# A Mamba-2 layer of a hybrid encoder: the splits of weight blocks are scheduled 140 instructions ahead instead of 60

## The chip, the cores and the metric

The kernel runs on one core of a Trainium2 chip, in one launch. The metric is the device time of one execution in microseconds (us). The engines are named as in the profile: PE (TensorE, with PEld for its weight loads), DVE (VectorE), ACT (ScalarE), POOL (GpSimd) and SP (SyncE, which here only issues transfers).

## The reference

The reference is an encoder trunk of two layers for one sequence of 512 tokens, 1024 wide, in float32. Layer 0 runs a bidirectional retention and a 2-D neighbourhood attention side by side, layer 1 a bidirectional Mamba-2 mixer; each layer ends with a GeGLU block. The mixer of layer 1, where the change is, computes per direction a chunked scan (chunks of 128 tokens, 4 groups of 8 heads, state 128):

```python
def step(h, inp):
    qq, kk, vv, aa = inp
    cs = jnp.cumsum(aa, axis=1)
    seg = cs[:, :, None] - cs[:, None, :]
    decay = jnp.exp(jnp.where(mask[None, :, :, None, None], seg, -jnp.inf))
    qk = jnp.einsum('bjgn,blgn->bjlg', qq, kk)
    y_intra = jnp.einsum('bjlgh,blghp->bjghp', qk[..., None] * decay, vv)
    y_inter = jnp.einsum('bjgn,bghnp->bjghp', qq, h) * jnp.exp(cs)[..., None]
    tail = jnp.exp(cs[:, -1:] - cs)
    h_new = h * jnp.exp(cs[:, -1])[..., None, None] + jnp.einsum('blgn,blghp->bghnp', kk, vv * tail[..., None])
    return h_new, y_intra + y_inter
```

Ahead of it stand a projection to z, x, B, C and the step sizes, a centred convolution of width 5 over x, B and C with a SiLU, and a softplus of the step sizes; behind it a gate with silu(z), a grouped RMSNorm and the output projection.

## The kernel before

Activations and weights are kept in two halves for PE's products in the type fp32r: `hi` is the cast of a float32 block, `lo` what the cast left over. A product of two blocks is three matmuls (`mm3`, L104 to L106): hi x hi, lo x hi, hi x lo. One of 512 columns starts every 0.22 us or so, and 24 of them (8 blocks of the 1024 rows, three each) make one tile of a projection.

A weight block comes in three steps. `wload` (L64) has SP load 128 x 1024 floats into a staging tile `wst`; `split` has ACT cast it to `whi` (L95) and VectorE subtract to `wlo` (L96). `wunit` does all three and puts the split into `tc.high_priority(60)`: the scheduler, which builds every engine's list of instructions at compile time, takes the two instructions as if they stood 60 instructions of the program earlier than where the kernel writes them. The load is not moved by that, it goes as early as its buffer allows. There are 3 staging buffers, 4 for high halves and 4 for low halves, and 4 accumulators `mm` and 4 small ones `px` in PSUM. An engine works through its list in order, so an instruction that waits holds up all that stand behind it.

`mixer1` is the Mamba-2 mixer. It works through four groups of 8 heads. The projection of a group has ten units: unit 0 is B, unit 1 is C, 2 to 5 are x, 6 to 9 are z. `project` makes a unit's weights, its 24 products, and for units under 6 the convolution: one ACT instruction (L754) and four of VectorE (L757). `silus` applies the SiLU to all tiles that are pending, the first as L763 (with a load of ACT's table if another function was in use), the rest as L766, and has B and x transposed by PE (L737, copied out by ACT at L738). For one group, `state` makes the state of one chunk and direction (VectorE L791, PE L793, ACT copies the first state of a direction at L796, VectorE L799 and L801 do the later ones); `head` turns one head's decays into a mask: ACT adds per-chunk offsets to a row of decays that a transfer has spread over the partitions (`pb`, L823, eight instructions), VectorE puts the other direction in by a copy under a mask (L825), ACT takes the exponential (L827) and issues the next load of `pb` (L812), and VectorE multiplies by the products of B and C (L829); `inter` and `pair` make the outputs (PE L844 and L864). The order of these pieces is written out by hand, one string per group (`SLOTS`): t is a unit of the own group, n one of the next, S and N their silus, s a state, h a head, i and p the outputs, o the output projection of the group before. Group 0 begins with

```python
"G s0 s1 t6 t7 s2 i0 h0 t8 t9 S h1 p0 i1 n0 h2 h4 h3 p1 i2 n6 n1 h5 n7 i3 n9 p2 N n3 n4 n2 n5 h6 h7 p3 n8 N",
```

Ahead of the groups, `mixer1` projects units 0 to 2 of group 0, calls `steps()`, and projects units 3, 4 and 5. `steps()` makes from the step sizes all that the scans need: a softplus as a polynomial on VectorE (L302 to L307), the running sum of the log decays (`pf`, a scan at L689), its exponentials on ACT (`ysc` and `sw`, L712 to L715), the table `tok` by PE transposes (L725) of two tiles, one with a logarithm (Ln, L720) and one the product `sw` (L717). It writes the running sums and `ysc` to DRAM (`pd`, L710, and `yd`, L716), and the loads of `pb` (the first three on SP, L812) and of `gain` (L836) read them back spread over the partitions. The numbers behind the names in the rows further down are the program's buffer numbers: whi_5978 holds the weights of n0 (unit 0 of group 1, projected in group 0's row of `SLOTS`), whi_6126 those of n1, whi_5860 and whi_5892 those of t8 and t9; mm_5982 is n0's accumulator and z_5921, z_5778, z_5810, z_5889 are the z tiles of group 0.

Of the kernel before, what the change touches and what calls it, by code (L numbers as in the profile page):

```python
# [26 lines left out]
class Env:  # L27


    def __init__(self, ctx, tc):  # L30
# [27 lines left out]
        self.xl = self.res.tile([P, KD, S], R32, name="xl")  # L58
        self.late, self.xs, self.turned = [], {}, {}

    def wload(self, src, behind=None):

        st = self.wst.tile([P, 1024], F32, name="wst")
        m = self.nc.sync.dma_start(st, src)  # L64
        if behind:
            self.together([m], [behind])
        return st

    def wunit(self, src, parts=None, st=None, behind=None, low_behind=None):

        if st is None:
            st = self.wload(src)
        halves = slice(0, 512), slice(512, 1024)
        if parts is None:
            hi, lo = self.whi.tile([P, 1024], R32, name="whi"), self.wlo.tile([P, 1024], R32, name="wlo")
            with self.tc.high_priority(60):
                self.split(hi, lo, st, behind, low_behind)
            return [(hi[:, c], lo[:, c]) for c in halves]  # L80
        with nullcontext() if behind else self.tc.high_priority(60):
            for j, c in enumerate(halves):
                self.split(parts[j], parts[j + 2], st[:, c], behind)
        return [(parts[j], parts[j + 2]) for j in range(2)]
# [537 lines left out]
def mixer1(E, w_dt, w_fm, cw, dtc, cols, mask, w_out, g_post_row, done, ahead):  # L622
# [8 lines left out]
    with ExitStack() as ctx:  # L631
# [102 lines left out]
        def to_tok(src, dst):  # L734
            pt = E.px.tile([P, NT, P], F32, name="pt", tag="px")
            for c in range(NT):
                nc.tensor.transpose(pt[:, c], src[:, c * C:(c + 1) * C], E.ident)  # L737
            nc.scalar.copy(dst, pt)  # L738
# [21 lines left out]
        def silus(o):  # L760

            r, src, i = o["silu"][-1]
            lead = nc.scalar.activation(r, src, AF.Silu)  # L763
            with tc.issue_after(lead.ins):
                for r, src, _ in o["silu"][:-1]:
                    nc.scalar.activation(r, src, AF.Silu)  # L766
            for r, _, i in o["silu"]:
                o["t"][i] = r
                if i == 0:
                    o["bt"] = one.tile([P, NT, P], F32, name="bt")  # L770
                    to_tok(r, o["bt"])
                elif 2 <= i < 6:
                    if "x" not in o:
                        o["x"] = two.tile([P, NT, 512], F32, name="xt")
                    to_tok(r, o["x"][:, :, (i - 2) * P:(i - 1) * P])
            o["silu"] = []

        def products(o):
            pg = E.px.tile([P, NT, P], F32, name="pg", tag="px")
            for c in range(NT):  # L780
                cc = slice(c * C, (c + 1) * C)
                nc.tensor.matmul(pg[:, c], o["t"][0][:, cc], o["t"][1][:, cc], start=True, stop=True)
            o["gt"] = one.tile([P, NT, P], F32, name="gt")
            nc.scalar.copy(o["gt"], pg)

        def state(o, dr, i):

            g = o["g"]
            c = i if dr == 0 else NT - 1 - i
            xs = E.tmp.tile([P, 512], F32, name="xs", tag="tmp")  # L790
            nc.vector.tensor_tensor(hv(xs), hv(o["x"][:, c]), rows(1, dr, g, c), op=ALU.mult)  # L791
            ps = E.px.tile([P, 512], F32, name="st", tag="px")
            nc.tensor.matmul(ps, o["bt"][:, c], xs, start=True, stop=True)  # L793
            ns = one.tile([P, 512], F32, name=f"state{dr}{i}")
            if i == 0:
                nc.scalar.copy(ns, ps)  # L796
            else:
                h = dr * H + g * HPG
                nc.vector.tensor_tensor(hv(ns), hv(o["st"][dr, i - 1]), etot[:, h:h + HPG, c:c + 1].broadcast_to([P, HPG, 64]),  # L799
                                        op=ALU.mult)  # L800
                nc.vector.tensor_tensor(ns, ps, ns, op=ALU.add)  # L801
            o["st"][dr, i] = ns
# [12 lines left out]
        def head(o, j):  # L815

            g = o["g"]
            h = g * HPG + j
            pb = pbs.pop(0)

            for dr in range(2):
                for c in range(NT):
                    nc.scalar.activation(pb[:, dr, c], pb[:, dr, c], AF.Identity, scale=1.0 - 2 * dr,  # L823
                                         bias=tok[:, 0, c, dr * H + h:dr * H + h + 1])
            nc.vector.copy_predicated(pb[:, 1], um.bitcast(U32).rearrange("p (o l) -> p o l", o=1).broadcast_to([P, NT, C]), pb[:, 0])  # L825
            e = three.tile([P, NT, C], F32, name="e")
            nc.scalar.activation(e, pb[:, 1], AF.Exp)  # L827
            load(nc.scalar)
            o["m"][j] = e, nc.vector.tensor_tensor(e, e, o["gt"], op=ALU.mult)  # L829

        def inter(o, q):

            g = o["g"]
            ysc = E.gain.tile([P, 2, S], F32, name="gain")
            for j in range(2):
                nc.sync.dma_start(ysc[j * 64:j * 64 + 64],  # L836
                                  yd.rearrange("(r h) s -> h r s", r=2)[g * HPG + 2 * q + j].partition_broadcast(64))
            y = ys.tile([P, S], F32, name="y")
            d, x = col[:, 0, g * 4 + q:g * 4 + q + 1], o["t"][2 + q]
            for dr in range(2):  # L840
                pi = E.px.tile([P, 3, C], F32, name="pi", tag="px")
                for i in range(NT - 1):
                    c = i + 1 if dr == 0 else NT - 2 - i
                    nc.tensor.matmul(pi[:, c - 1 + dr], o["st"][dr, i][:, q * P:(q + 1) * P],  # L844
                                     o["t"][1][:, c * C:(c + 1) * C], start=True, stop=True)
                cc = slice(C, S) if dr == 0 else slice(0, S - C)
                ti = E.tmp.tile([P, 384], F32, name="ti", tag="tmp")
                nc.vector.tensor_tensor(ti, pi.rearrange("p c l -> p (c l)"), ysc[:, dr, cc], op=ALU.mult)
                if dr == 0:
                    nc.vector.tensor_scalar(y[:, :C], x[:, :C], d, None, op0=ALU.mult)  # L850
                    nc.vector.scalar_tensor_tensor(y[:, cc], x[:, cc], d, ti, op0=ALU.mult, op1=ALU.add)
                else:
                    nc.vector.tensor_tensor(y[:, cc], y[:, cc], ti, op=ALU.add)
            o["yi"][q] = y
# [45 lines left out]
        def rms(o):  # L900

            if "ss" in o:
                E.together([nc.vector.tensor_tensor(o["ss"], squares(o, o["sq"][1], o["sqw"][3:]), o["ss"], op=ALU.add)], [o["yl"]])
            else:
                part(o)
            o["r"] = E.small.tile([P, NT], F32, name="rg", bufs=2)
            nc.gpsimd.tensor_tensor(o["r"], o["ss"], E.mhalf.broadcast_to([P, NT]), op=ALU.pow)
# [27 lines left out]
        def out(o, n):  # L935
            ws = E.wunit(w_out[o["g"], n, 0]) + E.wunit(w_out[o["g"], n, 1])
            for t in range(NT):
                out_tile(o, n, t, ws)
# [5 lines left out]
            silus(o)  # L944

        w0 = [E.wunit(w_fm[0, i]) for i in range(3)]
        p0 = [E.mm.tile([P, S], F32, name="mm") for _ in range(3)]
        for c in range(2):
            for i, (w, ps) in enumerate(zip(w0, p0)):
# [11 lines left out]
        for g, o in enumerate(gs):  # L961
            nx = gs[g + 1] if g + 1 < NG else None
            for step in SLOTS[g].split():
                a, i = step[0], int(step[1:] or 0)
                if a == "G":
                    products(o)
                elif a == "o":
                    out(gs[g - 1], i)
                elif a == "s":
                    state(o, 0, i)  # L970
                    state(o, 1, i)
                elif a == "h":
                    head(o, i)
                elif a == "i":
                    inter(o, i)
                elif a == "p":
                    pair(o, i)
                elif a == "R":
                    rms(gs[g - 1])
                elif a == "t":  # L980
                    project(o, i)
                elif a == "n":
                    project(nx, i)
                else:
                    silus(o if a == "S" else nx)
        g_post = E.bcast(g_post_row)
        st = {}

# [179 lines left out]
```

## Time and profile before

| | us |
|---|---|
| three timed runs | 1412.8, 1414.03, 1415.81 |
| median of them | 1414.03 |
| the profiled execution's own time | 1413.29 |
| its span in the trace | 1411.5 |
| PE busy in the span | 1386.6 |
| DVE, ACT, POOL busy | 905.2, 710.1, 61.3 |
| mixer1, from the trace | about 600 to 1020 |

The span is what the trace covers; the execution's own time is 1.8 us more. Rows of the timeline read: start, duration, engine, line, operation, what it writes and reads, count, and in brackets how long the engine sat idle before it and what ended that. PE's matmuls are pipelined, so their durations overlap and the distance of two starts tells how fast they go. SPq and ACTq are transfers issued by these engines, with the time that the issuing took.

### The profile page before, as it was taken

How to read it: one execution, taken by the hardware profiler on the slowest of the kernel's cores; microseconds unless marked ns; L12 is line 12 of the kernel's file. 1: busy time of each engine (PE TensorE's matmuls, PEld its weight loads, DVE VectorE, ACT ScalarE, POOL GpSimd, SP SyncE). 2: the span in 40 equal slices, each digit the busy share in tenths (PEclk: the TensorE clock that was granted, in tenths of full speed). 3: DMA queues.
4: the chain of work that ended last, by engine and by line, in shares of the span. 5: the costliest groups of instructions: out<-in, count | busy, mean ns of one | idle time of the engine just before them, and what ended most of it. 6: DMA issues, size and time to landing. Idle time of an engine off the chain costs nothing.

```text
span 1411.5 us, 18022 instructions
## 1 busy us (share of the span) xinstructions
PE 1386.6 (98%) x6908; PEld 1145.5 (81%) x6908; DVE 905.2 (64%) x1364; ACT 710.1 (50%) x1203; POOL 61.3 (4%) x66
## 2 busy tenths in 40 slices
PE   7999999999999999999999999999999999999998
PEld 6878787898888888888778787887888888888886
DVE  7378787755666552447878686897786565654232
ACT  5356665444444431334878787487354444442230
POOL 0010110100000000000000010000110000000000
PEclk9999999999999999999999999999999999999999
DMA  8442233223233333323566454273433323232231
GB/s 291 149 144 91 87 98 106 89 77 96 99 96 99 95 89 114 109 109 110 138 186 191 135 183 145 78 207 110 132 120 104 104 90 105 90 104 91 90 105 60
DMA packets 56439, 166.36 MB, mean 118 GB/s; under 512 B 6688, under 2 KB 7456, under 8 KB 56352
## 3 DMA queue, kind: packets, MB, share of 16 engines
q1 hardware_dynamic: 48464, 150.00, 33.3%
q10 hardware_dynamic: 7888, 15.21, 3.9%
q8 instruction: 55, 0.90, 0.3%
q14 instruction: 32, 0.26, 0.1%
HBM read 157.57 MB, written 5.51 MB: 116 GB/s over the span
## 4 chain that ended last, share of the span: by engine, by line
PE 90%; DVE 4%; ACT 3%; issue 1%; DMA 1%; POOL 0%; DVEq 0%; SPq 0%; POOLq 0%; ACTq 0%
PE mm L104 27%; PE mm L106 27%; PE mm L105 27%; PE pi L844 1%; PE st L793 1%; PE py L864 1%; PE pt L161 1%; PE pt L737 1%; PE y L519 1%; ACT pb L823 1%; DMA pb<-pd 0%; DMA x<-in_x 0%; DVE wlo L96 0%; ACT whi L95 0%; PE y L580 0%
## 5 line engine op out<-in xcount | busy, mean ns | idle before, releaser
L106 PE MATMUL mm<-xl,whi 128*128 128x512 f32 (+2 forms) x1216 | 463.9, 382 | 2.8 <-DVE xl L96 2.8
L104 PE MATMUL mm<-xh,whi 128*128 128x512 f32 (+1 forms) x1216 | 464.7, 382 | 0.7 <-ACT xh L95 0.2
L105 PE MATMUL mm<-xh,wlo 128*128 128x512 f32 (+2 forms) x1216 | 463.5, 381 | 1.2 <-DVE wlo L96 1.2
L96 DVE TENSOR_TENSOR wlo<-wst,whi 128x1024 fp32r<-128x1024 f32 (+1 forms) x208 | 255.2, 1228 | 136.7 <-ACT whi L95 134.8
L95 ACT CAST whi<-wst 128x1024 fp32r<-128x1024 f32 (+1 forms) x208 | 216.6, 1042 | 146.1 <-PE mm L105 117.7
L106 PEld LDWEIGHTS mm<-xl,whi 128*128 128x128 f32 (+1 forms) x1216 | 228.8, 188 | 47.3 <-DVE xl L96 3.0
L104 PEld LDWEIGHTS mm<-xh,whi 128*128 128x128 f32 x1216 | 229.1, 188 | 45.6 <-issue 2.5
L105 PEld LDWEIGHTS mm<-xh,wlo 128*128 128x128 f32 (+1 forms) x1216 | 229.1, 188 | 44.4 <-DVE wlo L96 1.6
L251 DVE SCALAR_TENSOR_TENSOR cv<-mm,cwt,cv 128x511 f32<-128x511 f32 x88 | 65.9, 749 | 147.1 <-ACT cv L250 147.1
L250 ACT ACTIVATE cv<-mm,cwt 128x512 f32<-128x512 f32 x88 | 68.6, 780 | 125.5 <-PE mm L106 125.5
L104 PE MATMUL mm<-whi,hh 128*128 128x512 f32 x288 | 112.0, 389 | 0.0
L105 PE MATMUL mm<-whi,hl 128*128 128x512 f32 x288 | 112.0, 389 | 0.0
L106 PE MATMUL mm<-wlo,hh 128*128 128x512 f32 x288 | 112.0, 389 | 0.0
L823 ACT ACTIVATE pb<-pb,tok 128x128 f32<-128x128 f32 x256 | 80.9, 392 | 8.4 <-DMA pb<-pd 6.4
L95 ACT CAST hh<-cv 128x512 fp32r<-128x512 f32 x44 | 27.3, 621 | 103.3 <-DVE cv L259 103.3
L252 DVE SCALAR_TENSOR_TENSOR cv<-mm,cwt,cv 128x511 f32<-128x511 f32 x88 | 66.0, 750 | 3.0
L105 PEld LDWEIGHTS mm<-whi,hl 128*128 128x128 f32 x288 | 54.1, 188 | 11.3
L104 PEld LDWEIGHTS mm<-whi,hh 128*128 128x128 f32 x288 | 54.1, 188 | 11.2
L106 PEld LDWEIGHTS mm<-wlo,hh 128*128 128x128 f32 x288 | 54.1, 188 | 11.2
L757 DVE SCALAR_TENSOR_TENSOR xf<-mm,cwt,xf 128x511 f32<-128x511 f32 (+1 forms) x64 | 47.5, 744 | 6.4 <-ACT xf L754 5.9
L96 DVE TENSOR_TENSOR hl<-cv,hh 128x512 fp32r<-128x512 f32 x44 | 30.5, 693 | 28.9 <-ACT hh L95 28.9
L141 ACT ACTIVATE junk<-mm 128x512 bf16<-128x512 f32 x24 | 14.3, 596 | 67.5 <-PE mm L106 67.4
(267 smaller groups left out, 1868.7 us busy)
## 6 DMA issues: line engine op xcount, KB each, us to landing
wst<-in_f_up SPq DMA_DIRECT2D x88, 512.0 KB
wst<-in_f_down SPq DMA_DIRECT2D x44, 512.0 KB
wst<-in_c_fm SPq DMA_DIRECT2D x40, 512.0 KB
pb<-pd ACTq DMA_DIRECT2D x29, 512.0 KB
wst<-in_ab_fm SPq DMA_DIRECT2D x20, 512.0 KB
gain<-yd SPq DMA_DIRECT2D x32, 256.0 KB
wst<-in_c_out SPq DMA_DIRECT2D x16, 512.0 KB
gain<-in_norms SPq DMA_DIRECT2D x8, 512.0 KB
```

The costliest lines, as they stand in the source:

```text
L95: first = self.nc.scalar.copy(hi, src)
L96: second = self.nc.vector.tensor_tensor(lo, src, hi.bitcast(F32), op=ALU.subtract)
L104: mm(out, lh, rh, start=first, stop=False)
L105: mm(out, ll, rh, start=False, stop=False)
L106: mm(out, lh, rl, start=False, stop=last)
L141: self.nc.scalar.activation(self.junk[:, :w], src, AF.Square, scale=float(n) ** -0.5, accum_out=s)
L161: last = nc.tensor.transpose(pt[:, j], xs[:, j * P:(j + 1) * P], self.ident)
L250: nc.scalar.activation(o, ps, AF.Identity, scale=w(1), bias=w(3))
L251: nc.vector.scalar_tensor_tensor(o[:, 1:], ps[:, :S - 1], w(0), o[:, 1:], op0=ALU.mult, op1=ALU.add)
L252: nc.vector.scalar_tensor_tensor(o[:, :S - 1], ps[:, 1:], w(2), o[:, :S - 1], op0=ALU.mult, op1=ALU.add)
L757: nc.vector.scalar_tensor_tensor(r[:, a], ps[:, b], wc(j), r[:, a], op0=ALU.mult, op1=ALU.add)
L823: nc.scalar.activation(pb[:, dr, c], pb[:, dr, c], AF.Identity, scale=1.0 - 2 * dr, bias=tok[:, 0, c, dr * H + h:dr * H + h + 1])
```

## The change

`Env` gets a field `lead`, 60 at first, and the split of a whole weight block goes ahead by `lead`. `mixer1` sets it to 140 behind the weights of its first three units and back to 60 behind the groups, before the output projection of the last group. So the weights of units 3 to 9 of group 0, all units of the other groups and the output projections of groups 0 to 2 are split with 140.

```diff
+        self.lead = 60
...
-            with self.tc.high_priority(60):
+            with self.tc.high_priority(self.lead):
                 self.split(hi, lo, st, behind, low_behind)
...
         w0 = [E.wunit(w_fm[0, i]) for i in range(3)]
+        E.lead = 140
         p0 = [E.mm.tile([P, S], F32, name="mm") for _ in range(3)]
...
                     silus(o if a == "S" else nx)
+        E.lead = 60
         g_post = E.bcast(g_post_row)
```

No work is added, and the only instructions that disappear are two of ACT's table loads (37 before, 35 after), which the new order makes unnecessary. Line numbers after the first edit are two higher than before. Below are the places where the order of ACT and VectorE changes most.

ACT while `steps()` is under way, before (xf_5694 and xf_5657 are x tiles of group 0 behind their convolution):

```order
L754 ACTIVATE xf_5694<-mm_5669,cwt_5201 128x512
L95 CAST whi_5892<-wst_5890 128x1024
L720 ACT_TABLE_LOAD
L720 ACTIVATE lp_e_5534<-lp_e_5534 128x256
L712 ACT_TABLE_LOAD
L712 ACTIVATE ysc_5475<-pf_5466 32x256
L699 ACTIVATE et_5513<-tot_5508 128x2
L712 ACTIVATE ysc_5475<-pf_5466 32x256
L95 CAST whi_5978<-wst_5976 128x1024
L715 ACTIVATE sw_5474<-pf_5466 32x256 x2
```

and after:

```order
L756 ACTIVATE xf_5694<-mm_5669,cwt_5201 128x512
L97 CAST whi_5892<-wst_5890 128x1024
L765 ACTIVATE xf_5694<-xf_5694 128x512
L768 ACTIVATE xf_5657<-xf_5657 128x512
L97 CAST whi_5978<-wst_5976 128x1024
L722 ACT_TABLE_LOAD
L722 ACTIVATE lp_e_5534<-lp_e_5534 128x256
L701 ACT_TABLE_LOAD
L701 ACTIVATE et_5513<-tot_5508 128x2
L714 ACTIVATE ysc_5475<-pf_5466 32x256 x2
L717 ACTIVATE sw_5474<-pf_5466 32x256 x2
```

The cast of n0's weights, which stood among the exponentials, is ahead of the logarithm and its table load, and so are the SiLUs of the two x tiles, which stood behind the exponentials.

VectorE at the same place, before (dt and la are the step sizes and log decays, xf_5694 the last x tile's convolution):

```order
L685 SCALAR_TENSOR_TENSOR dt_5473<-z_5464,lp_r_5480 128x256
L757 SCALAR_TENSOR_TENSOR xf_5657<-mm_5632,cwt_5201,xf_5657 128x510
L686 TENSOR_SCALAR la_5465<-dt_5473,bc_5460 128x256
L687 MEMSET msk_5476 128x256
L719 TENSOR_SCALAR lp_e_5534<-dt_5473 128x256
L688 MEMSET msk_5476 128x2
L757 SCALAR_TENSOR_TENSOR xf_5694<-mm_5669,cwt_5201,xf_5694 128x511
L689 SCALAR_TENSOR_TENSOR pf_5466<-msk_5476,la_5465 128x256
L757 SCALAR_TENSOR_TENSOR xf_5694<-mm_5669,cwt_5201,xf_5694 128x511
L693 COPY tot_5508<-pf_5466 128x2
L96 TENSOR_TENSOR wlo_5861<-wst_5858,whi_5860 128x1024
```

and after:

```order
L98 TENSOR_TENSOR wlo_5893<-wst_5890,whi_5892 128x1024
L309 TENSOR_TENSOR lp_r_5480<-lp_r_5480,lp_s_5478 128x256
L687 SCALAR_TENSOR_TENSOR dt_5473<-z_5464,lp_r_5480 128x256
L688 TENSOR_SCALAR la_5465<-dt_5473,bc_5460 128x256
L689 MEMSET msk_5476 128x256
L721 TENSOR_SCALAR lp_e_5534<-dt_5473 128x256
L690 MEMSET msk_5476 128x2
L98 TENSOR_TENSOR wlo_5979<-wst_5976,whi_5978 128x1024
L691 SCALAR_TENSOR_TENSOR pf_5466<-msk_5476,la_5465 128x256
L695 COPY tot_5508<-pf_5466 128x2
L698 TENSOR_TENSOR pf_5466<-pf_5466,la_5465 32x256 x2
```

The low half of n0's weights is now made before the scan, and those of t8 and t9 and the convolutions of both x tiles lie ahead of all these rows.

ACT from the first exponentials of heads to n0's convolution, before (e are the heads' masks, z the gates):

```order
L827 ACTIVATE e_5853<-pb_5559 128x512
L827 ACTIVATE e_5935<-pb_5561 128x512
...
L763 ACTIVATE z_5921<-mm_5896 128x512
...
L827 ACTIVATE e_6036<-pb_5855 128x512
L754 ACTIVATE bf_6007<-mm_5982,cwt_5201 128x512
L812 DMA pb_6038<-pd_5216 128x2x512
L823 ACTIVATE pb_5937<-pb_5937,tok_5214 128x128 x2
L95 CAST whi_6126<-wst_6124 128x1024
```

and after:

```order
L829 ACTIVATE e_5853<-pb_5559 128x512
L825 ACTIVATE pb_5563<-pb_5563,tok_5214 128x128
L814 DMA pb_5855<-pd_5216 128x2x512
L97 CAST whi_6126<-wst_6124 128x1024
L829 ACTIVATE e_5935<-pb_5561 128x512
L825 ACTIVATE pb_5563<-pb_5563,tok_5214 128x128
L814 DMA pb_5937<-pd_5216 128x2x512
L825 ACTIVATE pb_5855<-pb_5855,tok_5214 128x128 x2
L829 ACTIVATE e_6022<-pb_5563 128x512
...
L765 ACTIVATE z_5921<-mm_5896 128x512
```

The cast of n1's weights has moved from behind n0's convolution to between the first two exponentials, and two more steps on pb and one exponential now lie between the load of pb_5855 and the SiLU of the z tiles.

On SP eight loads of weights, for six before, stand ahead of the transfers of pd and yd; the three loads of pb come next behind those transfers, where one load of weights lay between.

## The prediction

> **What bounds the kernel now.** I read the page first, then PE's waits in the one stage that the change touches (the Mamba-2 mixer, about 600 to 1020 us), then windows, then the timeline of each engine where PE waits.
>
> ```profile
> span 1411.5 us, 18022 instructions
> ...
> PE 1386.6 (98%) x6908; PEld 1145.5 (81%) x6908; DVE 905.2 (64%) x1364; ACT 710.1 (50%) x1203; POOL 61.3 (4%) x66
> ...
> PE 90%; DVE 4%; ACT 3%; issue 1%; DMA 1%; POOL 0%; DVEq 0%; SPq 0%; POOLq 0%; ACTq 0%
> ```
>
> PE is busy 98% of the span and 90% of the chain that ended last. No instruction of PE is removed or added, so the change can act only through moments at which PE waits. PE's waits in the stage, as us in total, times, longest:
>
> ```profile
> PE mm L104 <- DVE xf L757: 1.4, 2, 1.2
> PE mm L105 <- DVE wlo L96: 1.2, 1, 1.2
> PE pt L725 <- DVE sw L717: 0.4, 1, 0.4
> PE mm L104 <- ACT xh L95: 0.2, 1, 0.2
> PE pss L891 <- POOL sq L876: 0.2, 1, 0.2
> PE mm L104 <- ACT z L763: 0.2, 1, 0.2
> ```
>
> All six come to 3.6 us, 0.25% of the span, and only one, 1.2 us, names a split's low half. That caps the gain: with every one gone the time falls by little more than the 0.2% (2.8 us) that a measurement of this kernel can tell from no change.
>
> **Part 1, what the change takes away: the wait near 727 us.** PE, then VectorE, then ACT:
>
> ```profile
> 726.27 0.39 PE L104 MATMUL mm<-xh,whi 128*128 128x512 f32 x1
> 727.87 0.50 PE L105 MATMUL mm<-xh,wlo 128*128 128x512 f32 x1 [1.21 <-DVE wlo L96]
> ```
>
> ```profile
> 723.58 3.10 DVE L757 SCALAR_TENSOR_TENSOR bf<-mm,cwt,bf 128x511 f32<-128x511 f32 x4
> 726.60 1.22 DVE L96 TENSOR_TENSOR wlo<-wst,whi 128x1024 fp32r<-128x1024 f32 x1
> ```
>
> ```profile
> 724.04 1.03 ACT L95 CAST whi<-wst 128x1024 fp32r<-128x1024 f32 x1
> ```
>
> The weights of unit n1 of group 0 are cast by 725.07, but VectorE holds the four convolution steps of n0's tile until 726.60, so PE's second product with these weights waits until 727.82. In the new order this cast (whi_6126) stands on ACT ahead of the second exponential of the first heads, of the z silus and of n0's convolution, and its subtraction moves with it. The buffer it takes is free once tile t8 is projected, and t8 and t9 lie ahead of n0, whose first product is at 715.26 (row below). So it is ready long before 726. From one product to the next it took 727.87 - 726.27 = 1.60, and would take 0.22 (two rows below): **-1.4 us.** What is late next there? The splits behind it, whi_6177 and whi_6228, are ahead of their old places too, and no row names another wait before 881; nothing is taken back here.
>
> **Part 2, what it puts in the way: the head of the stage, 680 to 716 us.** Here `steps()` turns the step sizes into decays on VectorE and ACT while PE projects tiles. The chain: the scan L689; the exponentials L712 to L715; the writes to pd and yd, and the product sw L717; PE's transpose L725 waits for sw, the pb loads L812 on SP for the writes, ACT's first work on pb for these loads; behind it on ACT are the state copies L796 and the z silus L763; the z silu frees the accumulator from which PE starts n0. Rows of PE, VectorE, SP and ACT:
>
> ```profile
> 683.69 0.39 PE L106 MATMUL mm<-xl,whi 128*128 128x512 f32 x1
> 683.91 0.39 PE L104 MATMUL mm<-xh,whi 128*128 128x512 f32 x1
> ...
> 689.24 0.44 PE L725 MATMUL pt<-head,sw 128*128 128x128 f32 x2 [0.35 <-DVE sw L717]
> ...
> 715.26 0.50 PE L104 MATMUL mm<-xh,whi 128*128 128x512 f32 x1 [0.17 <-ACT z L763]
> ```
>
> ```profile
> 681.79 0.68 DVE L689 TENSOR_TENSOR_SCAN pf<-msk,la 128x256 f32<-128x256 f32 x1
> ...
> 688.75 0.43 DVE L717 TENSOR_TENSOR sw<-sw,dt 128x256 f32<-128x256 f32 x1 [0.51 <-ACT sw L714]
> ```
>
> ```profile
> 687.96 0.59 SPq L716 DMA_DIRECT2D yd<-ysc  x1
> ...
> 690.09 1.43 SPq L812 DMA_DIRECT2D pb<-pd  x3
> ```
>
> ```profile
> 680.41 1.28 ACT L720 ACT_TABLE_LOAD   x1
> 681.70 0.42 ACT L720 ACTIVATE lp_e<-lp_e 128x256 f32<-128x256 f32 x1
> 682.14 1.28 ACT L712 ACT_TABLE_LOAD   x1
> 683.43 0.42 ACT L712 ACTIVATE ysc<-pf 32x256 f32<-32x256 f32 x1
> ...
> 684.41 1.05 ACT L95 CAST whi<-wst 128x1024 fp32r<-128x1024 f32 x1
> ...
> 687.23 0.41 ACT L713 ACTIVATE ysc<-tm 32x256 f32<-32x256 f32 x1
> ...
> 696.37 0.69 ACT L823 ACTIVATE pb<-pb,tok 128x128 f32<-128x128 f32 x2 [0.47 <-ACT xt L738]
> 696.97 0.56 ACT L784 COPY gt<-pg 128x512 f32<-128x512 f32 x1
> 697.44 1.28 ACT L823 ACTIVATE pb<-pb,tok 128x128 f32<-128x128 f32 x4
> ...
> 706.37 1.16 ACT L827 ACTIVATE e<-pb 128x512 f32<-128x512 f32 x2
> 707.03 0.95 ACTq L812 DMA_DIRECT2D pb<-pd  x2
> ...
> 712.86 0.40 ACT L823 ACTIVATE pb<-pb,tok 128x128 f32<-128x128 f32 x1 [2.25 <-DMA pb<-pd]
> ...
> 714.61 0.60 ACT L763 ACTIVATE z<-mm 128x512 f32<-128x512 f32 x1
> ```
>
> The new order puts the cast of n0's weights, whi_5978, ahead of the Ln table load on ACT, and its subtraction ahead of the scan on VectorE. Its buffer is the one from which tile t6 is multiplied; t6's last product is that at 683.69, over at 684.08. So both engines, which in the old order had Ln and scan done by 682.5, now stand still until then. Worked on from there:
>
> - ACT: cast 1.05 to 685.13, table 1.28 to 686.41, Ln 0.42 to 686.83, table 1.28 to 688.11. VectorE: subtraction 1.22 to 686.35, scan 0.68 to 687.03, in time for ACT's exponentials. From the end of the second table load to that of the last ysc took 687.64 - 683.42 = 4.22, of which 1.05 was the cast that now lies ahead: 3.17, so 691.28. The last write to yd was issued 0.32 after that: 691.6 for 687.96, **3.6 us later**.
> - PE and sw: the product sw moves from 688.75 to 692.35, ready at 692.8. PE comes to the transpose L725 13 products later in its own order (30 products of t7 and t8 ahead of it, where there were 17), 13 x 0.22 = 2.9, at 688.89 + 2.9 = 691.8, and waits 1.0 for the 0.35 before: **+0.65**.
> - The pb loads: issued at 690.09 + 3.6 = 693.7. Such a load took 712.86 - 707.03 = 5.83 from issue to its user where the row names the DMA as waited for; here at most 696.37 - 690.09 = 6.28. So pb is there at 699.5 to 700.0 and its first use moves from 696.37 by 3.1 to 3.6.
> - From there to the z silu on ACT: two of the small pb steps fewer before the first exponential (2 x 0.35, half of 0.69), one more before the next load is issued (+0.35), the gt copy gone to the front (-0.47, 696.97 to 697.44), and behind that load's landing two more small steps and one exponential (2 x 0.35 + 0.58, half of 1.16): together +0.5. The z silu is 3.6 to 4.1 late.
>
> So n0 and all behind it is later by 3.6 to 4.1 if the loads decide. The row at 696.37, though, names ACT's own copy and not the DMA: the data may have lain there for a while. If the loads don't decide, what is left is 0.65 at the transpose and some 0.25 on ACT, 0.9. I take **+3.6**: the only landing that a row shows as waited for is nearest to that. Both ends, 0.9 and 4.1, stay for the range.
>
> The Trainium skill, "DMA: Bandwidth & Descriptors", section "Anatomy of one DMA — SWDGE (gpsimd) path", fits a load as 2.0 us plus its bytes at 436 GB/s, which for pb's 512 KB gives an estimate of 3.2 us; by it pb would be there before ACT is free, the head would cost the lower 0.9, and the whole change -0.5 us. The trace shows 5.83 (707.03 to 712.86) for such a load from another queue, so the two differ by 2.6 us.
>
> **Part 3, the rest of the stage.** ACT loads its table twice less (35 in the program for 37, 1.28 each), at places where PE doesn't wait for ACT: nothing. At 881 PE waits 1.2 for the convolution of an xf tile (the first entry above). The new order puts one cast (1.05) ahead of that convolution on ACT; its subtraction (1.22) is then done before the convolution's last steps instead of among them, and these wait for a copy under a mask that is the same in both orders. Bounds: one cast later, +1.0, or the entry gone, -1.2; I take 0. Elsewhere the table names no wait for a split, and what the earlier splits displace is a row or two: 0.
>
> **Sum.** -1.4 + 3.6 + 0 = +2.2. The profiled execution took 1413.29 us, 0.74 under the median of the three runs (1414.03). In its own terms the changed kernel takes 1415.5, against the median 1414.03 + 2.2 = **1416.2**.
>
> **The rivals.**
>
> *Faster, or no change: the loads are hidden.* If pb lands before ACT asks for it, the head costs 0.9 and the sum is -1.4 + 0.9 = -0.5 (1413.5). If the waits at 881, for sw and for z go too (-1.2, -0.35, -0.17), it is -2.2; with all six entries gone and no new one, -3.6 (1410.4). For it: the 0.47 us at 696.37 are put down to a copy, and the skill's fit above says so too. Against it: the next pb load was waited for. Chance 0.27, of which 0.11 for a gain over 0.2%.
>
> *Slower: one stop long enough to lower the clock.* If PE is late by only 0.65 when it comes to n0 and the z silu by 4.1, PE stands still in one piece for 0.17 + 4.1 - 0.65 = 3.6 us. What a long stop costs:
>
> ```profile
> 1042.00 0.46 PE L106 MATMUL mm<-xl,whi 128*128 128x256 f32 x1 [2.81 <-DVE xl L96]
> ```
>
> ```profile
> 720.00:760.00 40.00, 38.79 (x207) 31.73 (x206) 32.51 (x44) 34.12 (x70) 2.60 (x2) 1.00 0.61 175
> ...
> 1041.00:1044.00 3.00, 2.00 (x10) 2.00 (x11) 2.90 (x6) 3.00 (x6) 0.54 (x1) 0.70 0.00 0
> 1044.00:1047.00 3.00, 3.00 (x21) 3.00 (x21) 3.00 (x7) 1.51 (x5) 0.21 (x1) 0.74 0.35 126
> ```
>
> With a stop of 2.81 us the granted clock (third number from the right) is 0.70 and 0.74 in two windows of 3 us, a loss of 0.9 + 0.8 = 1.7; with one of 1.21, in the window from 720, it stays 1.00. So it decides from some length between 1.2 and 2.8. Price: -1.4 + 4.1 + 1.7 = +4.4 (1418.4). The Trainium skill, "TensorE: Matmul & The Clock Gate", section "HAM oscillation — how this bites in real kernels", sets the point at gaps of about 3.4 us; the row of 2.81 with its 0.70 disagrees. Against this rival: the state copies behind pb hold PE up earlier and share the delay out. Chance 0.14.
>
> *Nothing moves in time.* The three staging buffers and four for high halves could hold each cast where it was, whatever the order says: 0, 1414.0. Against it: the buffer of whi_6126 is free before 715.26, and it was cast at 724.04. Chance 0.04.
>
> **How the numbers follow.** My forecast has 0.55, with a range of its own from -0.5 (the delay at 0.9) to +2.7 (at 4.1), and to +3.7 with one cast more at 881. Of the 0.55 I count 0.19 above +2.8, the rest within 0.2%. Faster than 1411.2: 0.11. Slower than 1416.9: 0.19 + 0.14 = 0.33. Between: 0.56. For 8 in 10 the range leaves out the far end of the first rival and, beyond +4.4, what could come to the second: 1411.8 (-2.2) to 1419.0 (+5).
>
> **What would show it.** In the profile after, line numbers are two higher. Part 1 is right if wlo is gone from PE's waits. Part 2 is right if the cast before the Ln table load stands still until 684 and the table load starts near 685.1, the scan after 686, the last yd write near 691.6, the first pb step at 699.5 to 700 with the DMA named, and n0 3.6 to 4.1 after 715.26. If the first pb step comes by 697.5, or n0 within 1 us of 715.26, the first rival holds. If a window from 715 to 723 shows a clock under 1.00, the second does. If the cast doesn't wait until 684, I have read its buffer wrong and all of part 2 falls.

## The result, and the profile after

The changed kernel takes 1415.73 us (median of 22 runs), the kernel before 1414.12 (22 runs beside them): a ratio of 1.0017, with a 95% interval from 1.0011 to 1.0022, so about 2.4 us slower. Of the page after:

```profile
span 1413.2 us, 18024 instructions
...
PE 89%; DVE 4%; ACT 2%; DMA 2%; issue 2%; POOL 0%; SPq 0%; DVEq 0%; POOLq 0%; ACTq 0%
```

The span is 1.7 longer, and transfers have 2% of the chain for 1%.

PE's waits between 600 and 1022 us in the profile after, as us in total, times, longest:

```profile
PE pt L727 <- DVE sw L719: 1.1, 1, 1.1
PE py L866 <- DVE e L831: 1.1, 1, 1.1
PE mm L106 <- ACT z L765: 1.0, 1, 1.0
PE mm L106 <- DVE xf L759: 0.9, 2, 0.7
...
```

The three rows left out have 0.2 each. The entry for wlo is gone, and the one for xf is shorter by 0.5. In their place stand 1.1 for the transpose of sw, 1.1 for the products e and 1.0 for the z silu: all three lie in the head of the stage.

To compare stages of two traces I take two instructions that both have: PE's first product of the mixer behind its inputs, and the sums of squares at the end of the groups. Before, then after:

```profile
647.92 0.39 PE L104 MATMUL mm<-xh,whi 128*128 128x256 f32 x1 [0.24 <-ACT xh L95]
...
1013.99 1.05 PE L891 MATMUL pss<-mean,sq 128*128 128x1 f32 x8 [0.19 <-POOL sq L876]
```

```profile
648.33 0.39 PE L106 MATMUL mm<-xh,whi 128*128 128x256 f32 x1 [0.24 <-ACT xh L97]
...
693.42 0.44 PE L727 MATMUL pt<-head,sw 128*128 128x128 f32 x2 [1.11 <-DVE sw L719]
...
714.82 1.09 PE L866 MATMUL py<-e,xt 128*64 128x128 f32 x16 [1.10 <-DVE e L831]
...
718.47 0.50 PE L106 MATMUL mm<-xh,whi 128*128 128x512 f32 x1 [1.02 <-ACT z L765]
...
1015.34 1.05 PE L893 MATMUL pss<-mean,sq 128*128 128x1 f32 x8 [0.19 <-POOL sq L878]
```

The stage takes 1013.99 - 647.92 = 366.07 before and 367.01 after, 0.94 more. n0's first product comes 67.34 into the stage before and 718.47 - 648.33 = 70.14 after: 2.80 late. Then the wait for wlo, 1.4, is not there, and the one at 881 is 0.5 shorter: 2.80 - 1.4 - 0.5 = 0.9. The rest of the 1.7 by which the span grew is 0.41 ahead of the stage and 0.35 behind it, where the two kernels' orders are the same.

ACT in the head, after:

```profile
683.59 0.63 ACT L765 ACTIVATE xf<-xf 128x512 f32<-128x512 f32 x1 [2.78 <-DVE xf L759]
...
684.65 1.04 ACT L97 CAST whi<-wst 128x1024 fp32r<-128x1024 f32 x1
685.71 1.28 ACT L722 ACT_TABLE_LOAD   x1
...
699.00 0.69 ACT L825 ACTIVATE pb<-pb,tok 128x128 f32<-128x128 f32 x2 [1.42 <-DMA pb<-pd]
...
712.62 0.64 ACT L829 ACTIVATE e<-pb 128x512 f32<-128x512 f32 x1 [1.68 <-DVE pb L827]
...
717.82 0.60 ACT L765 ACTIVATE z<-mm 128x512 f32<-128x512 f32 x1
```

Counted from the stage's first product the Ln table load is 4.9 later than before, the first step on pb 2.2 later and with the transfer named, the z silu 2.8 later. VectorE's row of the step sizes dt before, then VectorE and SP after:

```profile
679.45 0.41 DVE L685 SCALAR_TENSOR_TENSOR dt<-z,lp_r 128x256 f32<-128x256 f32 x1
```

```profile
685.20 0.42 DVE L687 SCALAR_TENSOR_TENSOR dt<-z,lp_r 128x256 f32<-128x256 f32 x1
...
687.54 0.68 DVE L691 TENSOR_TENSOR_SCAN pf<-msk,la 128x256 f32<-128x256 f32 x1
...
709.78 0.56 DVE L850 TENSOR_TENSOR ti<-pi,gain 128x384 f32<-128x384 f32 x1 [3.30 <-DMA gain<-yd]
```

```profile
693.90 1.42 SPq L814 DMA_DIRECT2D pb<-pd  x3
695.36 5.54 SPq L838 DMA_DIRECT2D gain<-yd  x4
```

dt is made 5.3 later in the stage, the scan behind it 5.3 too. The logarithm is late by another way as well: its input, made from dt, is ready at 686.43, but ACT comes to it only at 687.00, behind two SiLUs of x tiles that now stand ahead of it; the first of them waits 2.78 for VectorE's convolution (the row at 683.59). And far behind, at 709.78, VectorE waits 3.30 for a load of gain that was issued from 695.36 on. The chain that ended last, followed through this place, runs over that transfer (start, us, what):

```profile
696.81 12.78 DMA gain<-yd
```

### The profile page after: what moved, and what is told of

It reads as the page before. It is cut to its first block, busy times and chain, and to the rows that moved or that the text cites. A ratio compares the mean times of both kernels' runs of the same rounds, so it can differ in the third digit from the quotient of the medians.

```text
span 1413.2 us, 18024 instructions
## 1 busy us (share of the span) xinstructions
PE 1386.4 (98%) x6908; PEld 1145.3 (81%) x6908; DVE 905.8 (64%) x1364; ACT 707.5 (50%) x1201; POOL 61.4 (4%) x66
## 4 chain that ended last, share of the span: by engine, by line
PE 89%; DVE 4%; ACT 2%; DMA 2%; issue 2%; POOL 0%; SPq 0%; DVEq 0%; POOLq 0%; ACTq 0%
PE mm L106 27%; PE mm L108 27%; PE mm L107 27%; PE pi L846 1%; PE st L795 1%; PE py L866 1%; DMA gain<-yd 1%; PE pt L163 1%; DVE wlo L98 1%; PE y L521 1%; PE pt L739 1%; DMA pb<-pd 0%; DMA x<-in_x 0%; DVE xf L759 0%; PE y L582 0%
```

## The experiments

Theory A is the prediction's: the head of the stage is late, which costs more than the wait for wlo gives back. Its rivals at this point: B, the loss is spread over the stage; G, within the head it is the load of gain and not those of pb (P) that holds PE up last. Ratios are to the kernel before, timed beside each run; a stage's length is that between the two instructions above, in the one execution that was profiled. In the eleven traces the stage's difference from before and the one by the ratio differ by up to 2.4 us, so a stage's length alone does not show a gain or a loss of 1 us.

**One unit's lead.** Only unit 7 of group 0 is split with 140; by itself it brings the order of the head:

```diff
-        E.lead = 140
...
+                E.lead = 140 if (g, i) == (0, 7) else 60
                 w = E.wunit(w_fm[g, i])
+                E.lead = 60
```

> Only unit 7 of group 0 is split with 140, all others with 60. In this order the cast of n0's weights again stands ahead of the Ln table load and its subtraction ahead of the scan, and n1's cast again between the first two exponentials; the order from 730 us on is that of before. Theory A (the loss is the late head of the stage, 2.8 us at n0's first product; the gain is the wait for n1's low half, 1.4): n0's first product about 2.8 later than before, no wait for wlo near 727, 1.4 us over before in the span. Rival B (the loss is spread over the stage: more weight loads ahead of the small transfers everywhere, later swaps of casts and convolutions): with 63 of 64 splits at 60 the loss goes, and the time is that of before or up to 1.4 under it.

Ratio 1.0021 (1.0012 to 1.0030). PE's larger waits in the stage:

```profile
PE pt L727 <- DVE sw L719: 1.5, 1, 1.5
PE st L797 <- DVE xs L795: 1.4, 2, 1.1
PE mm L106 <- DVE xf L761: 0.9, 2, 0.7
...
```

n0 starts 69.48 into the stage, 2.1 late; no wait for wlo; the stage is 0.6 longer than before. B falls: the split of one weight block brings the loss. A was right in kind; the delay is 2.1 and not 2.8, since here the waits fall elsewhere (the states instead of py and z). This run also tells what makes the logarithm late: its table load comes 5.3 later in the stage than before, though dt is only 3.9 later, because ACT's SiLU again waits (3.17) for VectorE's convolution of the last x tile.

**The rest without the head.** 60 up to n0 of group 0, 140 behind it:

```diff
-        E.lead = 140
...
                     project(nx, i)
+                    if (g, i) == (0, 0):
+                        E.lead = 140
```

> 60 up to n0 of group 0, 140 behind it. The order of the head is that of before; n1's cast stands ahead of the z silus, and the casts further on stand as in the changed kernel. Theory A: n0's first product where it was before (715.3, give or take 0.4 of what lies ahead of the stage), no wait for wlo near 727 (-1.4), the wait at 881 us 0.5 shorter as in the changed kernel: 1.9 us under before. Rival B: the loss stays, 0 to 2 us over before.

Ratio 1.0001 (0.9992 to 1.0010), the stage 0.3 shorter. The head is in order and the wait for wlo gone, but A's 1.9 did not come, because a wait stands here that neither kernel has. PE, then ACT:

```profile
754.08 0.66 PE L739 MATMUL pt<-head,bf 128*128 128x128 f32 x4 [1.67 <-ACT bf L768]
```

```profile
749.97 0.69 ACT L825 ACTIVATE pb<-pb,tok 128x128 f32<-128x128 f32 x2 [3.70 <-DMA pb<-pd]
```

**100 instead of 140.**

```diff
-        E.lead = 140
+        E.lead = 100
```

> 100 in place of 140 at the same places. The head stands as before, n1's cast stands ahead of the z silus. Theory A: 1.4 us under before, n0's first product near 715.3, no wait for wlo near 727. Rival B (the further ahead, the more is lost): about half of the loss of 140, 0 to 1 us over before.

Ratio 1.0060 (1.0047 to 1.0072), 8.5 us slower: A and B both missed. The same wait is 5.0 us here, and a second one for a B tile, near 933, is 2.2. The first one, PE, then ACT:

```profile
758.23 1.12 PE L739 MATMUL pt<-head,bf 128*128 128x128 f32 x4 [5.02 <-ACT bf L768]
```

```profile
743.91 0.39 ACTq L814 DMA_DIRECT2D pb<-pd  x1
...
752.99 0.69 ACT L825 ACTIVATE pb<-pb,tok 128x128 f32<-128x128 f32 x2 [7.07 <-DMA pb<-pd]
...
757.56 0.62 ACT L768 ACTIVATE bf<-bf 128x512 f32<-128x512 f32 x1
```

The scheduler has put two steps on the first pb of group 1 ahead of the SiLUs that PE's transposes wait for. That pb is loaded only when an exponential has freed its buffer, at 743.91, and is first used 9.1 us later; ACT stands still for 7.07 of them. The wait brings a lower clock too (the column behind POOL's, granted clock, in 3 us windows):

```profile
758.00:761.00 3.00, 2.77 (x9) 2.38 (x10) 1.46 (x1) 3.00 (x6) 0.91 (x1) 0.50 0.55 175
761.00:764.00 3.00, 3.00 (x9) 2.32 (x8) 1.85 (x3) 2.99 (x5) 0.00 (x0) 0.53 0.21 57
```

So I added theory C: what these two runs lost at that place, they lost to ACT being held by steps on a pb that has not landed; against it D: splits further ahead crowd ACT in any order.

**Without the first load of gain.** The changed kernel, with the two transfers replaced by a fill with ones, so that the first pair's output lacks its factor; ACT, VectorE and PE keep the changed kernel's order:

```diff
+            if (g, q) == (0, 0):
+                nc.gpsimd.memset(ysc, 1.0)
-            for j in range(2):
+            for j in range(0 if (g, q) == (0, 0) else 2):
                 nc.sync.dma_start(ysc[j * 64:j * 64 + 64],
```

> The changed kernel, with the first pair's load of gain (its share of yd, 512 KB in two transfers) left out and the tile filled with ones by GpSimd instead: the factor on the first pair's output is not computed. ACT, VectorE and PE have the same order as in the changed kernel. Theory G (in the changed kernel the late load of gain holds VectorE 3.3 us, and with it the products e, PE's py and the z silu): VectorE's product ti no longer waits for a transfer, py's wait of 1.1 goes, the z silu comes 1.2 earlier, n0's first product at about 717.3 for 718.47, 1.2 us under the changed kernel. Theory P (the loads of pb set the z silu, as the prediction had it): the wait of py may go, but n0's first product stays within 0.3 of 718.47.

Ratio 1.0005 (0.9996 to 1.0014), 0.12% under the changed kernel's 1.0017; the two intervals overlap, so the time alone does not show a gain. The stage's first product is at 649.90 here, 1.6 later than in the changed kernel, so the 717.3 that G expected becomes 718.9. PE at n0, then ACT ahead of the z silu:

```profile
718.91 0.50 PE L106 MATMUL mm<-xh,whi 128*128 128x512 f32 x1 [0.95 <-ACT z L765]
```

```profile
715.33 0.69 ACT L825 ACTIVATE pb<-pb,tok 128x128 f32<-128x128 f32 x2 [2.29 <-DMA pb<-pd]
```

n0 is 69.01 into the stage where the changed kernel has 70.14: 1.1 earlier, and py's wait is gone. The stage takes 365.81, 1.2 less. G is right for 1.1 to 1.2 of the 2.8. The other 1.7 stay: the z silu now stands behind a load of pb that ACT issued at 709.72 and waits 2.29 for, and behind the two steps and the exponential that the new order puts there.

**All but units 7 and 8.** 140 as in the changed kernel, 60 for these two of group 0:

```diff
+                lead, E.lead = E.lead, 60 if g == 0 and i in (7, 8) else E.lead
                 w = E.wunit(w_fm[g, i])
+                E.lead = lead
```

> 140 everywhere as in the changed kernel, except units 7 and 8 of group 0 (60). The head then stands as before, n1's cast ahead of the z silus, and no step on group 1's first pb stands ahead of the SiLUs of group 1's B tile. Theory A with C (A: only the late head costs; C: the new wait of 1.7 and 5.0 us for the B tile near 753 in the runs with 60 up to n0 and with 100 is ACT held by two steps on a pb whose load has not landed): n0 where it was before, no wait for wlo near 727, no wait for the B tile's SiLU, 0.5 less at 881: 1.9 us under before in the stage. Rival D (any order with the splits further ahead pays a wait at the B tile, since the casts crowd ACT): 1.5 to 5 us of waiting near 753, 0 to 4 us over before.

Ratio 0.9988 (0.9978 to 0.9998). PE's waits in the stage are these three:

```profile
PE mm L106 <- DVE xf L761: 0.9, 2, 0.7
PE mm L106 <- ACT xh L97: 0.2, 1, 0.2
PE pss L895 <- POOL sq L880: 0.2, 1, 0.2
```

The stage takes 363.19, 2.9 less than before; the 1.9 of A with C came, and the small waits for sw and z (0.5 together) went as well; no wait explains the other 0.5. D falls here. n0's split itself has 140 in this run too, and the head stands as before: it is the splits of units 7 and 8 that change its order. With the head left alone, the change's idea gains a little, 0.12%.

**120, and 180.** The same line with 120 and with 180.

> 120 in place of 140. In the order the head stands almost as before, n1's cast ahead of the z silus, no step on group 1's first pb ahead of the B tile's SiLU. A with C: as with units 7 and 8 left at 60, 1.9 us under before, up to 1 less good if the two pd writes ahead of the yd writes shift the loads. Rival D: a wait for the B tile near 753, as with 100, and 2 to 8 us over before.

> 180 in place of 140. In the order the softplus's steps stand ahead of the scan almost as before, with the low half for t9 made earlier; n1's cast stands ahead of the z silus; no step on group 1's first pb stands ahead of the SiLU of group 1's B tile. A with C: head as before or up to 1.2 later, no wait for wlo near 727, none for the B tile: 0.7 to 1.9 under before. D (splits further ahead cost more): slower than the changed kernel.

With 120 the ratio is 1.0013 (1.0003 to 1.0023), with 180 it is 1.0020 (1.0011 to 1.0029): A with C missed both times (whether 180 is slower than 140, as D has it, these intervals do not tell). There is no wait for the B tile in either, so D's place is not it. PE and ACT with 120, then PE and ACT with 180:

```profile
720.87 0.50 PE L106 MATMUL mm<-xh,whi 128*128 128x512 f32 x1 [2.67 <-ACT z L765]
```

```profile
718.22 0.69 ACT L825 ACTIVATE pb<-pb,tok 128x128 f32<-128x128 f32 x2 [5.21 <-DMA pb<-pd]
```

```profile
700.17 7.08 PE L795 MATMUL st<-xs,bt 128*128 128x512 f32 x12 [2.09 <-DVE xs L793]
```

```profile
697.36 0.98 ACT L825 ACTIVATE pb<-pb,tok 128x128 f32<-128x128 f32 x3 [2.03 <-issue]
698.25 1.05 ACT L740 COPY xt<-pt 128x512 f32<-128x512 f32 x2
```

Both lose in the head after all. With 120 ACT stands still for 5.21 at two steps on a pb, with the z silu behind them: theory C in another place. With 180 three steps on a pb stand ahead of the copies xt, from which VectorE makes PE's xs; ACT is idle for 2.03 in front of them. The row names no transfer ("issue"), but the trace also keeps the moments at which each transfer raised its semaphore, part by part: for the first load of pb, issued at 691.46, the last one is 697.29, 0.07 ahead of these steps. So this is C once more. I had judged the head by the logarithm, the scan and the casts, and not by every step on pb in between.

**The steps on pb behind the SiLUs.** 100, and in the other kernel 60 up to n0 and 140 behind it, each with

```diff
             lead = nc.scalar.activation(r, src, AF.Silu)
+            o.setdefault("lead", lead)
...
+                  with tc.issue_after(o["lead"].ins) if (g, j) == (1, 0) else nullcontext():
                     nc.scalar.activation(pb[:, dr, c], pb[:, dr, c], AF.Identity, scale=1.0 - 2 * dr,
```

> 100 as in the run before, and ACT's steps on group 1's first pb told to go behind the first SiLU of group 1's B, C and z tiles. Nothing else is asked for; the rest of the order follows the scheduler. C: the wait of 5.0 us for the B tile falls under 1, and the clock there stays at 1.00, so 6 to 7 us under the run with 100, about 1.5 over before if the second wait of 2.2 near 933 stays, about 1 under before if it goes too. D (casts crowd ACT): 3 us or more of the wait stay.

> 60 up to n0 of group 0 and 140 behind it, and ACT's steps on group 1's first pb told to go behind the first SiLU of group 1's B, C and z tiles. A with C: the wait of 1.7 for the B tile goes, n0 where it was before, no wait for wlo: 1.9 us under before. D: 1 us or more of the wait stays, the time that of before.

With 100 the ratio goes from 1.0060 to 0.9988 (0.9977 to 0.9998), with 140 behind n0 from 1.0001 to 0.9992 (0.9982 to 1.0002). PE's waits with 100:

```profile
PE mm L106 <- DVE xf L759: 0.9, 2, 0.7
PE mm L106 <- ACT z L765: 0.7, 1, 0.7
PE pt L727 <- DVE sw L719: 0.4, 1, 0.4
...
```

The two rows left out have 0.2 each. The wait for the B tile is gone altogether, and so is the second one near 933; the stage is 364.44 for 373.01, 8.6 less. C is shown for the wait at the B tile: eight small steps on ACT, told to stand behind the first of the group's SiLUs, with what the scheduler rearranged behind them, are worth 0.7% of the kernel. The second wait went with that rearrangement; the steps that were moved do not stand there. So two orders (this one and 140 without units 7 and 8) beat the kernel before by 1.7 us, their intervals just clear of no change, and a third by 1.1, its interval not quite.

**n0's split behind the logarithm.** The changed kernel with

```diff
+                with tc.issue_after(gs[1]["ln"].ins) if (g, i) == (1, 0) else nullcontext():
                     w = E.wunit(w_fm[g, i])
```

> The changed kernel, with the split of n0's weights told to go behind the logarithm (Ln). Theory W (the prediction's: the head is late because this cast stands ahead of the Ln table load and its subtraction ahead of the scan, waiting for tile t6): the Ln table load starts near 681 to 682 as before, the scan near 682, the first pb step near 696.5, n0's first product near 715.5, and the time comes down by 2.5 to 3. Theory V (VectorE's own order: the convolutions of the last x tile and the low half for t9 now stand between the softplus's steps, so the step sizes are ready 5.7 later, and ACT's SiLUs ahead of Ln wait for those convolutions): only the cast's 1.05 and the subtraction's 1.15 go from the chain; the Ln table load starts near 684.7, the scan near 686.4, the first pb step near 698, n0 about 1 earlier than in the changed kernel, and the time comes down by about 1.

Ratio 1.0056 (1.0041 to 1.0070), far from both expectations. Its rows (the stage starts at 649.02, 0.7 later than in the changed kernel):

```profile
684.29 0.63 ACT L766 ACTIVATE xf<-xf 128x512 f32<-128x512 f32 x1 [2.80 <-DVE xf L760]
...
685.46 1.28 ACT L722 ACT_TABLE_LOAD   x1
...
715.59 0.98 ACT L826 ACTIVATE pb<-pb,tok 128x128 f32<-128x128 f32 x3 [4.05 <-DMA pb<-pd]
```

```profile
717.87 1.09 PE L867 MATMUL py<-e,xt 128*64 128x128 f32 x16 [4.08 <-DVE e L832]
```

Less 0.7 the table load is at 684.8, as V said and not as W said: without n0's cast ahead of it, it is only 0.9 earlier, and the logarithm, which then waits for VectorE, only 0.5. The time is lost further on, again by C: three steps on a pb that has not landed now stand ahead of an exponential (4.05), PE waits 4.08 for its product, and a wait of 2.8 for the B tile follows.

## Why the prediction was right, point by point

The forecast was +2.2 against the median; measured was +2.4 by the ratio, +1.6 by the medians, and the stage of the one profile shows +0.9. The likeliest case came: the head is late by more than the wait for wlo gives back, and loads carry the delay to n0. The step that was to start the delay was wrong, though, and that +2.4 lies so close to +2.2 is in part luck; the points below say how.

- **Part 1**: right. The wait for wlo is gone, -1.4.
- **Part 2, the size**: n0 came 2.8 late for the 3.6 taken, inside the bounds of 0.9 and 4.1. The pb loads stand where they were worked out (693.90 for 693.7), PE's wait for sw is 1.1 for 1.0, and the first step on pb names the DMA, which decides against the first rival. It came at 699.00 for 699.5 to 700, since this load took 5.10 from issue to use and not 5.83. In the kernel before the same load decided already: it raised its semaphore for the last time at 696.30, 0.07 ahead of the step at 696.37, whose row names a copy that had long been done. So the prediction's doubt about that row was needless, and its 6.28 was the load's time and not only a bound. The page "DMA: Bandwidth & Descriptors" of the Trainium skill, section "Anatomy of one DMA — SWDGE (gpsimd) path", gave an estimate of 3.2 for such a load, by a fit for transfers that GpSimd issues; these come from SP. The measurement stands between it and the row I used, nearer to the row.
- **Part 2, two steps that were wrong.** "Both engines ... now stand still until then" (until t6's last product): they did not wait for PE. ACT stood still for 2.78 until VectorE had finished the convolution of the last x tile, did two SiLUs from 683.59 on, and came to n0's cast at 684.65; VectorE was at work: the new order puts that convolution and the low half for t9 between the steps of the softplus, so dt is made at 685.20. That my time for the end of t6 (684.08) lay beside it is chance; the run with n0's split behind the logarithm shows that this cast carries 0.9 of the 4.9 us. I had read the rows right in front of the scan in the order, and not the twenty above them. No run puts only the two SiLUs back behind the exponentials, so how the delay is shared between them and VectorE's order is open. By the prediction's own words all of part 2 falls if the cast does not wait for t6; its chain behind the scan stood all the same, because VectorE's own work gave the scan about the same delay (5.3 for 5.2), which is luck. And "the loads decide" named only pb: of the 2.8 us, 1.1 to 1.2 go when the first load of gain is left out. It stands on SP behind the three pb loads, and VectorE waits 3.30 for it with the masks' products behind.
- **Part 3**: the wait at 881 fell by 0.5, inside the bounds; I took 0. This and the 0.8 of part 2 are why the stage lost 0.9 and not 2.2. That elsewhere nothing waits was right for this order, but not for reasons that the prediction had: with 100, or with 60 up to n0, the same stage has a wait of 1.7 to 5.0 that the profile before gives no hint of.
- **The rivals**: the hidden loads fell with the row at 699.00. The clock did not fall after PE's waits in the head; the longest is 1.1, since the delay was shared out as the prediction said. That nothing moves fell with the first row of the waits.
- What the profile's 0.9 in the stage lacks to the measured 2.4 is not settled. 0.4 us stand ahead of the stage and 0.4 behind it in this execution; runs of the changed kernel spread from 1414.0 to 1420.5, those of before from 1411.73 to 1416.17, and with loads now deciding at three places some of that may be their landing. Part of it may be that one trace is one execution: the stage's first product, ahead of which PE's order is the same in all twelve kernels, lies between 647.92 and 650.86 in the twelve traces. The clock is no likely cause: where it is on record, its mean is 0.998 over the runs of the one kernel and of the other. No run tells the rest apart.

## What to carry to other kernels

When a scheduler places prefetches, how far ahead is not one knob with an optimum: 60, 100, 120, 140 and 180 gave 1, 1.0060, 1.0013, 1.0017 and 1.0020, because each value shuffles the rest. With 100, 120, 140 and n0 behind the logarithm the trace names the same thing, and the question can be put to the order before a run: on an engine that works in order, does anything that waits for a transfer stand ahead of something the bound engine needs? With 180 the trace's semaphores show it too. The order alone does not answer the question, since it does not tell when the transfer lands: the expectations for 120, 180 and n0 behind the logarithm were read off the order and missed. Where the trace names such a piece, pinning it behind (8 instructions here) did more than any of the five values: 1.0060 became 0.9988. A pin shuffles the rest as well, though: the one on n0's split took 1.0017 to 1.0056.

## What the runs showed of the hardware

The stop of PE near 1040 to 1050, 2.75 to 2.82 us in ten of the twelve traces (2.52 in the other two), costs very different amounts. With 120, and in the run without the first gain load (granted clock behind POOL's column):

```profile
1044.00:1047.00 3.00, 1.09 (x9) 1.09 (x10) 2.90 (x5) 2.25 (x5) 0.54 (x1) 1.00 0.00 0
1047.00:1050.00 3.00, 3.00 (x28) 3.00 (x27) 3.00 (x6) 2.22 (x5) 0.00 (x0) 1.00 0.08 25
```

```profile
1044.00:1047.00 3.00, 2.90 (x13) 2.90 (x14) 2.90 (x6) 2.24 (x7) 0.54 (x1) 0.50 0.00 0
1047.00:1050.00 3.00, 3.00 (x16) 3.00 (x15) 2.57 (x6) 1.36 (x4) 0.92 (x1) 0.50 0.55 187
```

In the first the clock stays at 1.00 throughout; in the second it is 0.50 for both windows, a loss of about 3.0 us, and before it was 1.7. So a stop of one length can cost nothing or 3 us. Nor does the length order them. Behind the stop of 2.09 us with 180, and behind that of 2.67 us with 120, the windows have 0.56 and 1.00:

```profile
701.00:703.00 2.00, 2.00 (x4) 0.86 (x3) 2.00 (x5) 1.86 (x4) 0.00 (x0) 0.56 0.81 218
```

```profile
722.00:724.00 2.00, 2.00 (x11) 1.65 (x10) 1.06 (x3) 1.97 (x3) 0.00 (x0) 1.00 0.16 64
```

The prediction's "from some length between 1.2 and 2.8" is too simple. The page "TensorE: Matmul & The Clock Gate" of the Trainium skill says in its section "What's actually happening" that the window which decides runs free of the kernel; these rows fit that, though none shows the window. They do not fit a stop's length of about 3.4 us as the point, which the prediction took from the same page: 2.09 us was enough with 180.
